# Opening of a hybrid encoder block: the first products of one token block put ahead of the second block's transposes

## The chip, the core and the metric

The kernel runs on one core of a Trainium2 chip. The metric is the device time in microseconds of one execution. The core has a matrix engine (PE), a vector engine (DVE), a scalar engine (ACT), a general engine (POOL) and a queue engine (SP) that issues nearly all DMAs. Each engine works through its own list of instructions in order.

## What is computed

One layer of a streaming encoder over 2064 tokens (16 learned meta tokens, then 2048 inputs) of width 1024. The part that the change touches is the first line of it:

```python
p = rms_norm(h, norm_mix_pre[l]) @ w_in[l]      # h: (2064, 1024), w_in: 1024 x (512 + 1544 + 1024)
pa, pb, pc = ...                                 # columns of the three head groups
oa = rg_lru_group(...); ob = forgetting_attention_group(...); oc = rwkv7_group(...)
h = h + rms_norm(concat([oa, ob, oc]) @ w_out[l], norm_mix_post[l])
f = causal_dwconv(rms_norm(h, norm_ffn_pre[l]) @ ffn_up[l], ffn_conv[l])
h = h + rms_norm((gelu(gate) * val) @ ffn_down[l], norm_ffn_post[l])
```

`rms_norm` divides a token by the root of its mean square and multiplies by a gain. Among the columns of `w_in` are 8 for the gate of the attention group (`f_logit`).

## The kernel before

The input projection is done in three parts, each of two blocks of tokens; part 0 has the tiles of 16, 128, 128, 128 tokens (block 0, 400 tokens) and three tiles of 128 (block 1, 384 tokens). Products need the tokens turned, with the 1024 features on the partitions, and every operand is split into a high and a low half whose products are summed in three matmuls (`mm3`, lines 181 to 183).

`norm_transpose` brings one tile: a DMA into `xt` (line 131, tag `nt_x`, four buffers), the sum of squares on ACT (line 123, output to a throw-away tile `xj` of tag `stv`, two buffers), the reciprocal root by `rstd_from` on DVE (lines 90 to 92, then three rounds of lines 98 and 99, nine small instructions on one column), the scaling on DVE (line 136), eight transposes on PE (line 149, two PSUM tiles `pst`), and for each of these a copy on ACT (line 155, `xh`) and a subtraction on DVE (line 156, `xl`). With `core.root` set, `rstd_of` takes another way: two sums over half rows on ACT, one small DVE instruction, a square root on ACT (line 108) and a reciprocal on DVE (line 109). Before, it is set only in later stages.

`w_in_norm` does this for all seven tiles of part 0. Then `w_in_part` multiplies: first `w_in_gate` for both blocks (16 matmuls a block, lines 300 and 301, weights `fw` from the raw tile `fraw`, tag `stv`; `fw` lies in the pool `w` under the tag `wh`), then 24 units of 128 columns, each over both blocks (24 matmuls a block). `w_in_weights` loads a unit's columns in part 0 (`raw`, 512 KB, line 171, the same four `nt_x` buffers as the token tiles), rounds them on ACT (line 175) and subtracts on DVE (line 176), and stores both halves for the later parts (`scr_wk`, line 229). The pool `w` holds two units. Products are copied out of PSUM (lines 57 and 59) and stored (`scr_p`).

In program order the constants of the recurrences stand behind unit 12: `rwkv_consts`, `lru_consts` and the columns of `ffn_conv`, some 27 small DMAs on SP (lines 905, 952 to 955, 1442), among them the vectors that `columns` loads row by row into one tile `rows` (one buffer), turns on PE (line 911, `pscol`) and copies on DVE (line 912); that happens four times. But program order isn't what runs: the program is built with `schedule_with_timeline_sim=True`, so a planner orders each engine's instructions by its own simulated times, and it pulls the constants to the front. `tc.issue_after(ins)` keeps what is traced inside it behind `ins` on the engine of `ins`.

Of the kernel before, what the change touches and what calls it, by code (L numbers as in the profile page):

```python
# [8 lines left out]
F32 = mybir.dt.float32  # L9
F32R = mybir.dt.float32r  # L10
# [185 lines left out]
def w_in_norm(core, pools, psum, x, meta, gain, part):  # L196
    blocks = []
    for b, tl in enumerate(w_in_tokens(part)):
        t0 = tl[0][0]
        n = sum(r for _, r in tl)  # L200
        hi = pools["xn"].tile([P, KD, n], F32R, tag=f"xh{b}", name=core.n("xh"))
        lo = pools["xn"].tile([P, KD, n], F32R, tag=f"xl{b}", name=core.n("xl"))
        blocks.append((t0, n, tl, hi, lo))
    for t0, n, tl, hi, lo in blocks:
        for s, rows in tl:
            src = meta if s < META else x[s - META : s - META + rows, :]
            late = part == 1 and (s, rows) not in blocks[0][2][:2]
            after = (lambda: core.tc.issue_after(core.rounded.ins)) if late else nullcontext
            norm_transpose(core, pools, psum, src, rows, gain, [(hi, lo, s - t0, 0, rows)], after)
    return blocks  # L210


# [2 lines left out]
    return scr["wk"][c0 // P]  # L215


def w_in_weights(core, pools, w_in, c0, scr, part):

    if part == 0:  # L220
        src = w_in[:, c0 : c0 + P].rearrange("(k p) c -> p k c", p=P)
        pair = split_load(core, pools["w"], (pools["nt"], "nt_x", None), src, [P, KD, P], "w")
    else:
        core.turns += part == 2
        pl, tags = (pools["nt"], ("nt_x", "nt_x")) if core.turns % 4 > 1 else (pools["w"], ("wh", "wl"))
        pair = [pl.tile([P, KD, P], F32R, tag=tag, name=core.n(s)) for s, tag in zip(("wh", "wl"), tags)]
    for t, kept in zip(pair, w_in_kept(scr, c0)):
        t = t[:].rearrange("p k c -> p (k c)").bitcast(F32)
        core.loaded = core.nc.sync.dma_start(*((kept, t) if part == 0 else (t, kept)))
    return pair  # L230
# [51 lines left out]
def w_in_gate(core, pools, psum, w_in, blocks, scr, part):  # L282

    nc = core.nc
    c0 = 2048
    w = pools["w"].tile([P, KD, P], F32R, tag="wh", name=core.n("fw"))
    flat, kept = w[:].rearrange("p k c -> p (k c)").bitcast(F32), w_in_kept(scr, 3 * D)[0]
    if part == 0:
        raw = pools["st"].tile([P, KD, 8], F32, tag="stv", name=core.n("fraw"))
        nc.sync.dma_start(raw[:], w_in[:, c0 : c0 + 8].rearrange("(k p) c -> p k c", p=P))  # L290
        nc.vector.memset(w[:].bitcast(F32), 0.0)
        nc.scalar.activation(w[:, :, 0:8], raw[:], AF.Copy)
        nc.vector.tensor_tensor(w[:, :, 32:40], raw[:], w[:, :, 0:8], op=ALU.subtract)
        nc.sync.dma_start(kept, flat)
    else:
        nc.sync.dma_start(flat, kept)
    for t0, n, tl, hi, lo in blocks:
        ps = psum.tile([P, 512], F32, tag="mm", name=core.n("psf"))
        for k in range(KD):
            nc.tensor.matmul(ps[:, :n], w[:, k], hi[:, k], start=k == 0, stop=False)  # L300
            nc.tensor.matmul(ps[:, :n], w[:, k], lo[:, k], start=False, stop=k == KD - 1)
        a = pools["st"].tile([8, 400], F32, tag="sth", name=core.n("fa"))
        nc.scalar.activation(a[:, :n], ps[32:40, :n], AF.Copy)
        o = pools["st"].tile([8, 400], F32, tag="stl", name=core.n("fo"))
        nc.vector.tensor_tensor(o[:, :n], ps[0:8, :n], a[:, :n], op=ALU.add)
        nc.sync.dma_start(scr["f"][:, t0 : t0 + n], o[:, :n])
    yield False
    yield True


def w_in_part(core, pools, psum, w_in, blocks, scr, part):
    yield from w_in_gate(core, pools, psum, w_in, blocks, scr, part)
    units = [("c", 2056 + P * i) for i in range(8)] + [("a", P * i) for i in range(4)]
    units += [(s, c + P * i) for s, c in (("k", 1024), ("v", 1536), ("q", 512)) for i in range(4)]
    waiting = [None]

    def step(*args):

        after = w_in_step(core, pools, psum, *args, scr)
        if waiting[0]:  # L320
            waiting[0]()
        waiting[0] = after

    for kind, c0 in units[:-2]:
        w = w_in_weights(core, pools, w_in, c0, scr, part)
        for block in blocks:
            step(w, block, kind, c0)
            yield block is blocks[-1]

    last = [(w_in_weights(core, pools, w_in, c0, scr, part), kind, c0) for kind, c0 in units[-2:]]  # L330
    for block in blocks:
        for w, kind, c0 in last:
            step(w, block, kind, c0)
            yield kind == "q" and c0 == last[-1][2]
# [1821 lines left out]
def hybrid_block_kernel(ctx: ExitStack, tc: tile.TileContext, args, out):  # L2156
# [12 lines left out]
    def pool(es, name, bufs, **kw):  # L2169
        return es.enter_context(tc.tile_pool(name=name, bufs=bufs, **kw))  # L2170
# [11 lines left out]
    with ExitStack() as p1:  # L2182
# [8 lines left out]
        with ExitStack() as p1a:  # L2191
            ps_mm = pool(p1a, "ps_mm", 5, space=PSUM)
            g_pre = spread(pool(p1a, "gpre", 1), a["norm_mix_pre"], "g_pre")
            pools = {"xn": pool(p1a, "xn", 1), "nt": pool(p1a, "nt", 4), "w": pool(p1a, "w", 2), "st": pool(p1a, "st", 2)}
            sums = up_sums(core, pool(p1a, "us", 1), a["ffn_up"], scr, EARLY)
            split_out = w_out_split(core, pools["nt"], a["w_out"], scr)
            following = w_in_norm(core, pools, ps_mm, x, meta, g_pre, 0)
            for part in range(3):
                blocks = following
                if part == 0:  # L2200
                    zeros = pools["st"].tile([P, PAD], F32, tag="sth", name="zeros")
                    nc.vector.memset(zeros[:], 0.0)
                    for r in range(0, A_ROWS + C_ROWS, P):
                        nc.gpsimd.dma_start(scr["p"][r : r + P, 0:PAD], zeros[:])
                units = w_in_part(core, pools, ps_mm, a["w_in"], blocks, scr, part)
                for _ in range(READY if part == 0 else 0):
                    while not next(units):
                        pass
                if part == 0:
                    attn_consts(core)  # L2210
                    shared, core.const = core.const, rc
                    rk = rwkv_consts(
                        core, gp, ps_ae,
                        {
                            s[5:]: (v.rearrange("h d -> (h d)") if s == "rwkv_r_k" else v)
                            for s, v in a.items() if s.startswith("rwkv_")
                        },
                    )
                    lk = lru_consts(
                        core, gp, ps_ae,  # L2220
                        {
                            "conv_w": a["lru_conv_w"], "conv_b": a["lru_conv_b"], "ga_w": a["lru_gate_a_w"],
                            "ga_b": a["lru_gate_a_b"], "gx_w": a["lru_gate_x_w"], "gx_b": a["lru_gate_x_b"],
                            "lam": a["lru_lambda"],
                        },
                    )
                    core.const = shared
                    columns(core, gp, ps_ae, [a["ffn_conv"].rearrange("i (r p) -> (i r) p", p=P)], "", cw)
                    R = Rwkv(core, rp, dp, ps_rw, ps_ae, scr, rk)
                    beside = Beside(PACE)  # L2230
                i = READY + 1 if part == 0 else 1
                for whole in units:
                    if whole and i == READY + 1:
                        beside.add(recurrences(core, R, lk, a["fox_f_bias"], scr, blocks, part))
                    beside.advance()
                    if not whole:
                        continue
                    if part == 1 and i > 1:
                        next(split_out, None)
                    if part and i % 2 == 0:  # L2240
                        with tc.issue_after(core.loaded.ins):
                            next(sums, None)
                    i += 1
                run(sums) if part == 2 else None
                if part < 2:
                    following = w_in_norm(core, pools, ps_mm, x, meta, g_pre, part + 1)
# [199 lines left out]
```

## Time and profile before

| | us |
|---|---|
| three runs | 2972.48, 2979.31, 2978.02 |
| their median | 2978.02 |
| the profiled execution | 2974.88 |
| its span | 2973.2 |
| PE busy in the span | 2840.2 |
| DVE, ACT, POOL busy | 2015.4, 1505.3, 1281.3 |

The profile's page gives the busy time of each engine, a row of 40 slices of the span, the chain that ended last, and groups of instructions with their mean duration and the idle time of their engine just before them. The timeline lists instructions in order of time, with the idle time before each and what ended it in brackets. A granted clock of TensorE stands beside each stretch.

### The profile page before, as it was taken

The page shows a single profiled execution, that of the slowest core. Times are in us where ns is not written, and L with a number is a line of the kernel's source. Part 1 is how long each engine was busy: PE and PEld are TensorE (multiplying, and loading weights), DVE is VectorE, ACT ScalarE, POOL GpSimd, SP SyncE. Part 2 cuts the span into 40 slices and gives each one's busy share as a digit, 9 for nine tenths or more (in the row PEclk, how much of TensorE's full clock was granted, in tenths as well). Part 3 has the DMA queues.
Part 4 walks back from the last instruction along what each step waited for, and adds up shares of the span by engine and source line. Part 5 has one row for each costly group of instructions (what it writes and reads, how often), then busy time and mean ns, then how long its engine had stood idle before and what let it go on. Part 6 is the DMA issues. An engine that isn't in the chain of part 4 may idle for free.

```text
span 2973.2 us, 53343 instructions
## 1 busy us (share of the span) xinstructions
PE 2840.2 (96%) x18854; PEld 2448.6 (82%) x18854; DVE 2015.4 (68%) x3974; ACT 1505.3 (51%) x2937; POOL 1281.3 (43%) x1555
## 2 busy tenths in 40 slices
PE   6999999999978889999999999999999999999998
PEld 6998899889865555566568999999999999787887
DVE  5257654675678766556756988888778787646766
ACT  4246432444346555445635665666575665324333
POOL 1001121131214566766722667455655444656443
PEclk9999899999989899999999999999999999999999
DMA  6776479576654257535245665577777774436453
GB/s 219 235 233 223 156 246 322 171 240 213 209 127 95 70 130 215 125 95 130 72 133 187 204 191 173 167 230 211 205 212 219 218 199 131 155 114 222 148 171 121
DMA packets 470344, 530.52 MB, mean 178 GB/s; under 512 B 86862, under 2 KB 356888, under 8 KB 468524
## 3 DMA queue, kind: packets, MB, share of 16 engines
q1 hardware_dynamic: 469308, 526.18, 58.4%
q8 instruction: 148, 2.42, 0.3%
q14 instruction: 120, 0.98, 0.1%
q0 software_dynamic: 768, 0.93, 0.1%
HBM read 368.07 MB, written 158.90 MB: 177 GB/s over the span
## 4 chain that ended last, share of the span: by engine, by line
PE 72%; DVE 8%; DMA 7%; ACT 5%; POOL 4%; issue 3%; SPq 1%; DVEq 0%; POOLq 0%; ACTq 0%
PE psu L181 9%; PE psu L182 9%; PE psu L183 9%; PE psp L183 5%; PE psp L182 5%; PE psp L181 5%; PE psd L181 4%; PE psd L182 4%; PE psd L183 4%; PE po L733 3%; PE sc L710 2%; PE pswo L181 2%; PE pswo L182 2%; PE pswo L183 2%; PE mx L581 2%
## 5 line engine op out<-in xcount | busy, mean ns | idle before, releaser
L182 PE MATMUL psu<-xo,uw 128*128 128x344 f32 x1848 | 591.5, 320 | 0.0
L181 PE MATMUL psu<-xo,uw 128*128 128x344 f32 x1848 | 586.0, 322 | 3.5 <-DVE vb L1907 2.1
L183 PE MATMUL psu<-xo,uw 128*128 128x344 f32 x1848 | 581.9, 320 | 0.3 <-DVE uw L1716 0.3
L181 PE MATMUL psp<-xh,wh 128*128 128x384 f32 (+2 forms) x1152 | 378.3, 328 | 0.1
L183 PE MATMUL psp<-xh,wl 128*128 128x384 f32 (+2 forms) x1152 | 377.0, 328 | 0.7 <-DMA wl<-scr_wk 0.7
L182 PE MATMUL psp<-xl,wh 128*128 128x384 f32 (+2 forms) x1152 | 377.6, 328 | 0.0
L1716 DVE TENSOR_TENSOR uw<-uq,uw 128x512 fp32r<-128x512 f32 x341 | 318.8, 940 | 61.3 <-ACT uw L1715 58.3
L181 PEld LDWEIGHTS psu<-xo,uw 128*128 128x128 f32 x1848 | 345.8, 188 | 5.1 <-DVE vb L1907 3.1
L182 PEld LDWEIGHTS psu<-xo,uw 128*128 128x128 f32 x1848 | 347.2, 188 | 0.0
L183 PEld LDWEIGHTS psu<-xo,uw 128*128 128x128 f32 x1848 | 345.7, 188 | 1.1 <-DVE uw L1716 1.1
L1715 ACT ACTIVATE uw<-uq 128x512 fp32r<-128x512 f32 x462 | 288.1, 627 | 100.1 <-PE psu L183 47.3
L715 ACT ACTIVATE p<-sc,bias 128x512 f32<-128x512 f32 (+4 forms) x352 | 196.4, 590 | 166.8 <-PE sc L711 141.9
L586 DVE TENSOR_REDUCE mc<-mx 128x1 f32<-128x512 f32 (+5 forms) x352 | 191.8, 566 | 119.4 <-PE mx L581 82.9
L1855 DVE SCALAR_TENSOR_TENSOR uy<-psu,ffn_cols,uy 128x342 f32<-128x342 f32 (+1 forms) x390 | 220.6, 567 | 62.4 <-ACT uy L1853 60.7
L1716 POOL TENSOR_TENSOR uw<-uq,uw 128x512 fp32r<-128x512 f32 x121 | 184.1, 1521 | 136.7 <-ACT uw L1715 112.9
L1863 POOL TENSOR_TENSOR uy<-uy,uy 128x342 f32<-128x342 f32 (+1 forms) x132 | 144.2, 1092 | 228.7 <-DVE uy L1855 63.1
L183 PEld LDWEIGHTS psp<-xh,wl 128*128 128x128 f32 x1152 | 219.9, 191 | 7.1 <-issue 4.6
L181 PEld LDWEIGHTS psp<-xh,wh 128*128 128x128 f32 x1152 | 219.8, 191 | 4.5 <-issue 2.6
L182 PEld LDWEIGHTS psp<-xl,wh 128*128 128x128 f32 x1152 | 220.0, 191 | 3.7 <-issue 2.3
L754 POOL TENSOR_TENSOR acc<-acc,p 128x512 f32<-128x512 f32 (+3 forms) x186 | 196.5, 1059 | 48.5 <-DVE acc L754 21.4
L1716 DVE TENSOR_TENSOR fo<-u,fo 128x896 fp32r<-128x896 f32 x88 | 100.3, 1140 | 133.0 <-ACT fo L1715 132.4
L1715 ACT ACTIVATE fo<-u 128x896 fp32r<-128x896 f32 x88 | 81.2, 923 | 207.6 <-PE psd L183 122.3
(489 smaller groups left out, 6301.5 us busy)
## 6 DMA issues: line engine op xcount, KB each, us to landing
uq<-scr_us SPq DMA_DIRECT2D x220, 256.0 KB
uq<-in_ffn_up_dram SPq DMA_DIRECT2D x209, 256.0 KB
wl<-scr_wk SPq DMA_DIRECT2D x48, 512.0 KB
wh<-scr_wk SPq DMA_DIRECT2D x48, 512.0 KB
u<-scr_ff SPq DMA_DIRECT2D x88, 256.0 KB
scr_ff<-uy SPq DMA_DIRECT2D x110, 171.0 KB
raw<-in_w_in_dram SPq DMA_DIRECT2D x24, 512.0 KB
scr_wk<-wh SPq DMA_DIRECT2D x24, 512.0 KB
```

The source lines that it names most:

```text
L181: nc.tensor.matmul(out, ah, bh, start=first, stop=False, skip_group_check=more)
L182: nc.tensor.matmul(out, ah, bl, start=False, stop=False, skip_group_check=more)
L183: nc.tensor.matmul(out, al, bh, start=False, stop=last, skip_group_check=more)
L581: nc.tensor.matmul(ps[:rows, : e - a], q3[:, qo : qo + rows], k2[:, a:e], start=True, stop=not last)
L586: self.reduced = nc.vector.tensor_reduce(mc[:rows, i, ci : ci + 1], ps[:rows, : e - a], axis=AX.X, op=ALU.max)
L715: last = nc.scalar.activation(p[:rows, :w], ps[:rows, :w], AF.Exp, bias=bias[:rows, j : j + 1])
L733: mm = nc.tensor.matmul(po[at : at + 64, c0:n], v1[:rows, j], p[:rows, : n - c0], start=start and i < 2, stop=end and i + 2 >= len(group), ...
L754: eng.tensor_tensor(a, ps_[0][0][:rows, c0:n] if start and i == 1 else a, p[:rows, : n - c0], op=ALU.add)
L1715: core.nc.scalar.activation(hi, src, AF.Copy)
L1716: (eng or core.nc.vector).tensor_tensor(lo, src, hi, op=ALU.subtract)
L1855: core.conved = stt(y[:, :n], src[:, i : n + i], cw[:, 44 * i + cc : 44 * i + cc + 1], y[:, :n], op0=ALU.mult, op1=ALU.add)
L1863: core.pooled = nc.gpsimd.tensor_tensor(v[:, :n], g[:, :n], v[:, :n], op=ALU.mult)
```

## The change

- Block 0 of part 0 is normalised and turned first. The three tiles of block 1 are put on a list (`core.unturned`), and `core.turn_tile` does one of them: after unit 0's product with block 0, after unit 1's, and the third behind that. Then come the gate and the two units for block 1, and the other 22 units as before.
- The raw columns of units 0 and 1 go to a tile of their own (`rw_e` of the pool `rp`, which the recurrence uses later) instead of the `nt_x` buffers; the gate's weights go to the pool `us` instead of a `wh` buffer, so that `w` holds both units.
- `core.root` is set for the seven tiles of part 0.
- The SP instructions of the constants are put behind the last `scr_wk` store of unit 3.

```diff
 def w_in_norm(core, pools, psum, x, meta, gain, part):
...
+    core.unturned = []
+    for block in blocks:
+        for s, rows in block[2]:
+            if part == 0 and block is blocks[1]:
+                core.unturned.append((block, s, rows))
+            else:
+                tile(block, s, rows)
+    core.turn_tile = lambda: tile(*core.unturned.pop(0))
     return blocks
...
-def w_in_weights(core, pools, w_in, c0, scr, part):
+def w_in_weights(core, pools, w_in, c0, scr, part, raw=None):
+
+    src = w_in[:, c0 : c0 + P].rearrange("(k p) c -> p k c", p=P)
+    if raw is not None:
+        pair = hi, lo = [pools["w"].tile([P, KD, P], F32R, tag=s, name=core.n(s)) for s in ("wh", "wl")]
+        core.loaded = core.nc.sync.dma_start(raw, src)
+        core.rounded = core.nc.scalar.activation(hi[:], raw, AF.Copy)
+        core.nc.vector.tensor_tensor(lo[:], raw, hi[:], op=ALU.subtract)
+    elif part == 0:
...
 def w_in_gate(core, pools, psum, w_in, blocks, scr, part):
...
-    w = pools["w"].tile([P, KD, P], F32R, tag="wh", name=core.n("fw"))
+    home, tag = ("w", "wh") if part else ("us", "us")
+    w = pools[home].tile([P, KD, P], F32R, tag=tag, name=core.n("fw"))
...
 def w_in_part(core, pools, psum, w_in, blocks, scr, part):
...
+    if part == 0:
+        raws = pools["rp"].tile([P, 2, KD, P], F32, tag="rw_e", name=core.n("raw"))
+        firsts = [
+            (w_in_weights(core, pools, w_in, c0, scr, part, raws[:, i]), kind, c0)
+            for i, (kind, c0) in enumerate(units[:2])
+        ]
+        for i, block in enumerate(blocks):
+            gate(*block)
+            yield i > 0
+            for w, kind, c0 in firsts:
+                step(w, block, kind, c0)
+                if i == 0:
+                    core.turn_tile()
+                yield i > 0
+            while core.unturned:
+                core.turn_tile()
+        del units[:2]
...
+            core.root = True
             following = w_in_norm(core, pools, ps_mm, x, meta, g_pre, 0)
...
-                for _ in range(READY if part == 0 else 0):
+                for i in range(READY if part == 0 else 0):
                     while not next(units):
                         pass
+                    core.root = core.root and not i
+                    if i == 4:
+                        begun = core.loaded.ins
                 if part == 0:
                     attn_consts(core)
                     shared, core.const = core.const, rc
+                    p1c = ExitStack()
+                    p1c.enter_context(tc.issue_after(begun))
                     rk = rwkv_consts(
...
+                    p1c.close()
                     R = Rwkv(core, rp, dp, ps_rw, ps_ae, scr, rk)
```

More of the change, by code (lines that the diff above doesn't have):

```diff
@@ L203, in w_in_norm, with tile @@
         blocks.append((t0, n, tl, hi, lo))
[L204 to L209, printed above, removed]
+    def tile(block, s, rows):
+        t0, _, _, hi, lo = block
+        src = meta if s < META else x[s - META : s - META + rows, :]
+        late = part == 1 and (s, rows) not in blocks[0][2][:2]
+        after = (lambda: core.tc.issue_after(core.rounded.ins)) if late else nullcontext
+        norm_transpose(core, pools, psum, src, rows, gain, [(hi, lo, s - t0, 0, rows)], after)
+    core.unturned = []
[6 more added lines that the diff above has]
+    core.turn_tile = lambda: tile(*core.unturned.pop(0))
     return blocks
@@ L215, in w_in_kept @@
     return scr["wk"][c0 // P]
-def w_in_weights(core, pools, w_in, c0, scr, part):
-    if part == 0:
-        src = w_in[:, c0 : c0 + P].rearrange("(k p) c -> p k c", p=P)
+def w_in_weights(core, pools, w_in, c0, scr, part, raw=None):
[6 more added lines that the diff above has]
+    elif part == 0:
         pair = split_load(core, pools["w"], (pools["nt"], "nt_x", None), src, [P, KD, P], "w")
@@ L296, in w_in_gate, with products @@
         nc.sync.dma_start(flat, kept)
-    for t0, n, tl, hi, lo in blocks:
+    def products(t0, n, tl, hi, lo):
         ps = psum.tile([P, 512], F32, tag="mm", name=core.n("psf"))
@@ L306, in w_in_gate @@
         nc.sync.dma_start(scr["f"][:, t0 : t0 + n], o[:, :n])
-    yield False
-    yield True
+    return products
 def w_in_part(core, pools, psum, w_in, blocks, scr, part):
-    yield from w_in_gate(core, pools, psum, w_in, blocks, scr, part)
+    gate = w_in_gate(core, pools, psum, w_in, blocks, scr, part)
     units = [("c", 2056 + P * i) for i in range(8)] + [("a", P * i) for i in range(4)]
@@ L322, in step @@
         waiting[0] = after
+    if part == 0:
[15 more added lines that the diff above has]
+        del units[:2]
+    else:
+        for block in blocks:
+            gate(*block)
+        yield False
+        yield True
     for kind, c0 in units[:-2]:
@@ L2194, in hybrid_block_kernel @@
             pools = {"xn": pool(p1a, "xn", 1), "nt": pool(p1a, "nt", 4), "w": pool(p1a, "w", 2), "st": pool(p1a, "st", 2)}
-            sums = up_sums(core, pool(p1a, "us", 1), a["ffn_up"], scr, EARLY)
+            pools["us"], pools["rp"] = pool(p1a, "us", 1), rp
+            sums = up_sums(core, pools["us"], a["ffn_up"], scr, EARLY)
             split_out = w_out_split(core, pools["nt"], a["w_out"], scr)
+            core.root = True
             following = w_in_norm(core, pools, ps_mm, x, meta, g_pre, 0)
```

## The prediction

> **What bounds the kernel now.** I read the page's busy shares first, then its 40 slices, then stretches of the opening, and last the timelines of single engines there.
>
> ```profile
> span 2973.2 us, 53343 instructions
> PE 2840.2 (96%) x18854; PEld 2448.6 (82%) x18854; DVE 2015.4 (68%) x3974; ACT 1505.3 (51%) x2937; POOL 1281.3 (43%) x1555
> PE   6999999999978889999999999999999999999998
> ```
>
> PE is the bound: of 133 us without PE work, the first slice (74 us at six tenths) holds the largest single share, 23 by the next view. Time saved there by PE moves everything behind it. The stretches of the opening, and two later ones (columns: length, then busy us and instructions of PE, PEld, DVE, ACT, POOL, granted clock, DMA share, GB/s):
>
> ```profile
> 0.00:33.40 33.40, 9.95 (x44) 7.91 (x44) 26.15 (x134) 15.08 (x29) 11.94 (x32) 1.00 0.62 185
> 33.40:36.60 3.20, 3.15 (x16) 2.92 (x17) 3.11 (x10) 1.39 (x3) 0.00 (x0) 1.00 1.05 400
> 36.60:60.00 23.40, 23.40 (x134) 23.40 (x133) 10.20 (x24) 12.91 (x19) 0.00 (x0) 1.00 0.73 224
> 280.00:300.00 20.00, 10.94 (x247) 9.95 (x245) 15.88 (x50) 16.25 (x34) 5.54 (x12) 0.72 0.68 216
> 300.00:320.00 20.00, 19.02 (x142) 15.83 (x143) 17.80 (x43) 13.74 (x28) 4.87 (x9) 0.59 0.08 24
> ```
>
> From 33.4 us on PE is full. Before it PE works 9.95 of 33.4 us, on transposes and constants alone. What PE waits for there:
>
> ```profile
> 10.36 1.00 PE L149 MATMUL pst<-ident,xt 16*128 16x16 f32 x8 [10.36 <-DVE rs L99]
> 12.77 0.27 PE L911 MATMUL pscol<-ident,rows 22*128 22x22 f32 x1 [1.41 <-DMA rows<-in_rwkv_ln_b_dram]
> 13.82 1.97 PE L149 MATMUL pst<-ident,xt 128*128 128x128 f32 x8 [0.78 <-DVE xt L136]
> 18.02 0.26 PE L911 MATMUL pscol<-ident,rows 16*128 16x16 f32 x1 [2.23 <-DMA rows<-in_lru_lambda_dram]
> 18.20 1.97 PE L149 MATMUL pst<-ident,xt 128*128 128x128 f32 x8
> 22.90 1.94 PE L149 MATMUL pst<-ident,xt 128*128 128x128 f32 x8 [2.73 <-DVE xt L136]
> ...
> 33.45 3.42 PE L149 MATMUL pst<-ident,xt 128*128 128x128 f32 x16 [4.51 <-DVE lruv L1456]
> 36.62 0.43 PE L300 MATMUL psf<-xh,fw 128*128 128x400 f32 x1
> ```
>
> Block 0 is the first four groups of line 149; the fourth ends at 24.8 us, yet the first product starts at 36.62, behind all seven tiles. What holds the tiles is seen on ACT:
>
> ```profile
> 7.19 1.06 ACT L123 ACTIVATE xj<-xt 128x1024 bf16<-128x1024 f32 x1 [0.41 <-DMA xt<-in_x_dram]
> ...
> 10.73 1.06 ACT L123 ACTIVATE xj<-xt 128x1024 bf16<-128x1024 f32 x1 [0.42 <-DMA xt<-in_x_dram]
> 11.69 0.18 ACT L123 ACTIVATION_READ_ACCUMULATOR xj<-xt 128x1 f32 x1
> 11.78 0.32 ACT L155 ACTIVATE xh<-pst 128x64 fp32r<-128x64 f32 x2
> 17.34 1.06 ACT L123 ACTIVATE xj<-xt 128x1024 bf16<-128x1024 f32 x1 [5.24 <-DMA xt<-in_x_dram]
> 18.40 1.06 ACT L155 ACTIVATE xh<-pst 128x512 fp32r<-128x512 f32 x2
> ```
>
> All four tiles of block 0 have landed by 10.73. Then ACT sits 5.24 us in front of the fifth tile, a block 1 tile, while tile 1, turned at 15.8, waits for its copy until 18.40. The chain of waits says why that tile is late:
>
> ```profile
> 3.13 7.92 DMA rows<-in_rwkv_mu_dram
> ...
> 13.60 3.64 DMA xt<-in_x_dram
> ```
>
> A 4 KB vector issued at 3.13 landed at 11.05, behind the tokens: SP's transfers pass in order, and the constants stand in SP ahead of the fifth tile, which is issued at 13.60 and needs 3.64 us.
>
> **The change, part by part.** Prices from the groups of the opening and of the stage that already takes roots on ACT:
>
> ```profile
> L136 DVE SCALAR_TENSOR_TENSOR xt<-xt,rs,g_pre 128x1024 f32<-128x1024 f32 x5 | 6.4, 1273 | 0.0
> L156 DVE TENSOR_TENSOR xl<-pst,xh 128x512 fp32r<-128x512 f32 x8 | 5.4, 682 | 0.1
> L155 ACT ACTIVATE xh<-pst 128x512 fp32r<-128x512 f32 x8 | 4.4, 584 | 1.6 <-PE pst L149 1.6
> L98 DVE SCALAR_TENSOR_TENSOR rs<-rs 128x1 f32<-128x1 f32 x17 | 3.5, 216 | 0.0
> L99 DVE SCALAR_TENSOR_TENSOR rs<-rs 128x1 f32<-128x1 f32 x17 | 2.6, 157 | 0.0
> L175 ACT ACTIVATE wh<-raw 128x1024 fp32r<-128x1024 f32 x1 | 1.1, 1057 | 0.4 <-DMA raw<-in_w_in_dram 0.4
> L1610 ACT ACTIVATE jk<-pswo 128x512 bf16<-128x512 f32 x17 | 10.0, 588 | 8.9 <-PE pswo L183 8.5
> L1610 ACT ACTIVATION_READ_ACCUMULATOR jk<-pswo 128x1 f32 x17 | 3.3, 195 | 0.0
> L108 ACT ACTIVATE rs<-rs x25: 276/285/297, 1534.8 to 2967.9; 128x1 f32<-128x1 f32 x25
> L108 ACT ACT_TABLE_LOAD  x3: 1283/1283/1283, 1533.5 to 2760.2; - x3
> L911 PE MATMUL pscol<-ident,rows 22*128 22x22 f32 (+3 forms) x4 | 1.2, 308 | 3.7 <-DMA rows<-in_lru_lambda_dram 2.2 <-DMA rows<-in_rwkv_ln_b_dram 1.4
> L176 DVE TENSOR_TENSOR wl<-raw,wh 128x1024 fp32r<-128x1024 f32 x1 | 1.2, 1226 | 0.3 <-ACT wh L175 0.3
> L1051 ACT ACTIVATE rwwa<-rwraw,rwkv_om x3: 503/507/512, 114.8 to 242.0; 128x256 f32<-128x256 f32 x3
> ```
>
> (1) *Roots on ACT.* DVE loses three rounds of 0.216 + 0.157 = 1.1 us a tile; the three small instructions ahead of them become one and a reciprocal. ACT's squares grow from 1.06 + 0.18 to 2 x (0.588 + 0.195) = 1.57 us, and it gets a root of 0.285 and one table load of 1.283, which falls on tile 0. ACT thus does more, 0.6 us a tile; only the shorter chain on DVE pays.
>
> On that load the Trainium skill has a harder rule: "ScalarE: Activation LUTs", section "What ACT_TABLE_LOAD costs", says that a switch to another set costs 1283 ns and a drain of about 1380 more. The rows show the 1.283 alone, with the root beginning right behind it (1533.5 to 1534.8). With the page's drain the sum below would be 1.4 us less.
>
> (2) *When does block 0 stand?* I go along ACT. Tile 0's squares begin when the meta tokens land; tile 3 lands at 10.73 unless the raw weights pass before it. After 10.73 the shortest way is: squares 1.57, root and reciprocal with hand-overs 0.7, scaling 1.27, transposes 1.97, the last copy 0.58, the last subtraction 0.68, and some 0.1 for each of five hand-overs: 18.0. ACT is also behind by then: the work in front of tile 3's squares pushes them by some 2 us (table load 1.28, three roots 0.85), so 19.5 as the near end. The far end has the copies of tiles 1 and 2 (4 x 0.58) and unit 0's rounding (1.06) in front of tile 3's root: 3.4 later, 22.9. I take the middle, 21. The raw weights ahead of the tokens would cost two tile steps (7.19 to 10.73 is two tiles, 3.5 us), which the far end holds. `fraw` needs the throw-away buffer of tile 2's squares, so it is issued at about 12 and lands behind two raws by some 18 to 19, in time.
>
> (3) *What PE has to do from there.* At 33.45 two tiles were left to turn (3.42 us); at 21 three are (3 x 1.95 = 5.85): 2.4 us more. The four `pscol` transposes, 1.2 us, lay in PE's idle time and now lie in the full stretch. So 33.45 - 21 - 2.4 - 1.2 = 8.8 us; with the two ends of (2), 10.3 and 6.9.
>
> (4) *Block 1.* Matmuls pass every 23.40/134 = 0.175 us, so the gate (16) and two units (48) over block 0 give 11.2 us of cover: until 32 at the earliest. Tile 4's buffer is free at 11.4 (tile 0 turned), those of 5 and 6 about 3 and 5 us later; with 3.64 us to land and two raws and `fraw` in front, tile 6 lands by about 23 and is scaled by 27. Cover 5 us, cost nothing; without it, up to the 5.24 us that ACT once sat.
>
> (5) *Weights.* Units 0 and 1 keep both halves of `w` until block 1's products are done. Unit 2's rounding and subtraction (1.06, and 1.23 on DVE) then run beside unit 1 over block 1 (24 x 0.175 = 4.2 us): nothing, unless its raw tile is late; it is loaded some 15 us ahead. The gate's move to `us` and the raws' to `rp` use buffers that nobody wants before part 1 and the recurrences: nothing. The 2.5 MB of stores to `scr_wk` come some 12 us earlier, and SP, in order, holds whatever stands behind a store that waits for its halves; what stands there are raws of units 2 and later, early by more than 10 us.
>
> (6) *Constants.* SP's 27 small issues move behind unit 3's store. Unit 3's half comes free when both first units are through: 21 + 11.2 + 5.85 + 11.2 = 49, and the rounding and subtraction make it about 52 us. The first reader of them is at 114.8 (line 1051), so 40 us of cover remain after some 20 us for the batch. Behind them in SP queue the raws of units 5 and on (four buffers, over 25 us ahead) and `scr_p` stores (two buffers and five PSUM tiles). The price is on PE: a `pscol` transpose stands in PE's list and everything behind it waits if its rows are late. Before, the waits were 1.41 and 2.23 and about nothing, 3.7 us on an idle PE. Bounds: 0, if the planner places them late enough, and 3.7. I take 1.4, nearer to nothing, since the batch is now small between large transfers and PE has other work ready.
>
> Sum: 8.8 - 1.4 = 7.4 us, between 6.9 - 3.7 = 3.2 and 10.3. Against the profiled execution, 2974.88, that gives 2967.5. The median of the three runs is 2978.02, 3.1 us above it; against it the time is 2970.6.
>
> **Rivals.** About 0.2% (6 us) is what a measurement here can tell from none.
>
> *A. ACT is held again, now by a raw tile or tile 4 in front of block 0's copies.* For it: the 5.24 us above, which came from the planner putting the fifth tile's squares before tile 1's copy. Against: constants no longer stand in front of that tile. One such wait takes 5.24 off: 2.2 us gained, 2975.8.
>
> *B. Slower: the constants stop a full PE.* Place: the four `pscol` in PE's list at 52 to 80 us. Price: if each load takes what the first one took, 7.92, and nothing covers it, 31.7 - 8.8 = 22.9 slower, 3001. It decides from 8.8 + 6 = 14.8 us of waits in all, 3.7 each. For it: SP passes in order, and 0.73 of the DMA time is taken there; against: the waits before were 1.41 and 2.23.
>
> *C. More than forecast.* PE's three earlier groups show that DVE's queue, not only ACT, held tiles (2.73 <-DVE xt, 4.51 <-DVE lruv); with constants gone it may be quick throughout. Block 0 at 18.0 and no `pscol` wait: 33.45 - 18 - 3.6 = 11.8, 2966.2, and with two roots earlier some 13, 2965.
>
> *D. The clock.* After the gap at 280 to 300 the granted clock is 0.72 and then 0.59; in the opening it is 1.00 although PE idles 10.36 us there. If the products, which now follow a sparse stretch instead of 3.42 us of dense transposes, ran their first 3.4 us at half clock, 1.7 us would go: 2972.3.
>
> The rule beside D is that of the Trainium skill, "TensorE: Matmul & The Clock Gate", section "Part 1: The HAM clock gate (the "warmup" mystery)": after an idle window of about 3.4 us the clock halves until a busy window has passed. The opening's rows speak against it, the later ones for it.
>
> **How the numbers follow.** The forecast has 0.60 (2967.7 to 2974.8 on its own bounds; three quarters or more of it beyond 6 us), A 0.12, B 0.10, C 0.13, D 0.05. Faster by over 0.2%: most of the forecast, 0.51, and C, 0.13: 0.64. Within 0.2%: the rest of the forecast 0.09, A and D: 0.26. Slower: B, 0.10. The range holds the forecast, A, C and D and half a spread of the runs above A: 2963 to 2979.
>
> **What would show it.** Right: the first `psf` at about 21 us with PE full from there; no waits of ACT on `xt` over 1 us ahead of block 0's copies; roots at 8 to 15 us with one table load; `pscol` at 55 to 80 us with less than 2 us of PE idle in all; units 2 and on without a wait for `wl`. Wrong: a PE wait at the seam between unit 1 over block 0 and the gate over block 1, `pscol` waits above 3.7 each, or the stages behind 100 us in another order with another length of the hole at 280 to 300.

## The result, and the profile after

The changed kernel took 2987.89 us (median of 17 runs), the kernel before in the same session 2978.10: ratio 1.0029, with a 95% interval from 1.0018 to 1.0040. It is 9.8 us slower. The forecast of 2970.6 was wrong in size and in sign.

The busy shares and PE's slices of the page after, as shown of before:

```profile
span 2988.6 us, 53295 instructions
PE 2858.3 (96%) x18854; PEld 2460.5 (82%) x18854; DVE 2015.5 (67%) x3925; ACT 1511.2 (51%) x2960; POOL 1288.6 (43%) x1555
PE   7999999999978889999999999999999999999998
```

The span grew by 15.4 us and PE's busy time by 18.1, with the same 18854 matmuls: PE did not wait more in sum, its matmuls took longer. The first slice rose from 6 to 7: the opening did gain, and the loss lies elsewhere.

I followed the same matmuls of PE through both timelines, by their count within each product. In the median the changed kernel is 3.2 us ahead over 55 to 135 us. At 865 us that lead is gone (between 1.3 us ahead and 2.2 behind, by product); from 910 us it is behind by about 12, from 1240 us to the end by 13 to 15. Three places matter.

**The opening.** PE's timeline after:

```profile
20.73 0.70 PE L317 MATMUL psf<-xh,fw 128*128 128x400 f32 x1
21.23 0.54 PE L181 MATMUL psp<-xh,wh 128*128 128x400 f32 x1
...
24.62 0.42 PE L181 MATMUL psp<-xh,wh 128*128 128x400 f32 x1
24.88 0.34 PE L182 MATMUL psp<-xl,wh 128*128 128x400 f32 x1
...
29.97 1.03 PE L149 MATMUL pst<-ident,xt 128*128 128x128 f32 x8
...
35.22 1.91 PE L149 MATMUL pst<-ident,xt 128*128 128x128 f32 x16
...
41.17 0.45 PE L317 MATMUL psf<-xh,fw 128*128 128x384 f32 x1 [4.05 <-ACT xh L155]
...
42.48 0.69 PE L181 MATMUL psp<-xh,wh 128*128 128x384 f32 x1 [0.68 <-DVE xl L156]
43.08 0.69 PE L318 MATMUL psf<-xl,fw 128*128 128x384 f32 x1
...
48.36 0.47 PE L181 MATMUL psp<-xh,wh 128*128 128x384 f32 x1
48.67 0.34 PE L182 MATMUL psp<-xl,wh 128*128 128x384 f32 x1
```

The first product starts at 20.73 (forecast: 21). The last tile of block 0 had its root on ACT at 14.39, but its scaling on DVE came behind the subtraction for unit 1's weights:

```profile
16.40 1.21 DVE L235 TENSOR_TENSOR wl<-raw,wh 128x1024 fp32r<-128x1024 f32 x1
17.54 1.28 DVE L136 SCALAR_TENSOR_TENSOR xt<-xt,rs,g_pre 128x1024 f32<-128x1024 f32 x1
```

At the seam of the two blocks PE waits 4.05 us for ACT's copies. ACT's timeline shows what held them:

```profile
6.99 1.28 ACT L108 ACT_TABLE_LOAD   x1
8.29 0.29 ACT L108 ACTIVATE rs<-rs 16x1 f32<-16x1 f32 x1
...
35.37 0.63 ACT L453 ACTIVATE rwr<-rwk,fb 8x400 f32<-8x400 f32 x1 [3.67 <-DMA rwk<-scr_f]
36.01 1.28 ACT L454 ACT_TABLE_LOAD   x1
37.31 0.54 ACT L454 ACTIVATE rwr<-rwr 8x400 f32<-8x400 f32 x1
37.86 1.28 ACT L455 ACT_TABLE_LOAD   x1
39.15 0.54 ACT L455 ACTIVATE rwr<-rwr 8x400 f32<-8x400 f32 x1
39.60 2.00 ACT L155 ACTIVATE xh<-pst 128x512 fp32r<-128x512 f32 x4
```

Lines 453 to 455 are the further work on the gate of block 0. They come earlier with the gate's product, wait 3.67 us for a DMA, load two tables, and the four copies of block 1's last two tiles stand behind them.

**The constants.** Their issues on SP begin at 62 us; the transposes on PE come far later, and so does the first reader of them (line 1091, 1051 before). One row each from SP's timeline and from the views of the tiles `pscol` and `rwwa`:

```profile
62.43 0.94 SPq L945 DMA_DIRECT2D rows<-in_rwkv_mu_dram  x1
L951 PE MATMUL pscol<-ident,rows x4: 220/232/272, 142.4 to 165.1; 22*128 22x22 f32 x1, 16*128 16x16 f32 x1, 128*128 128x128 f32 x1, 4*128 4x4 f32 x1
L1091 ACT ACTIVATE rwwa<-rwraw,rwkv_om x9: 348/508/510, 143.4 to 889.9; 128x256 f32<-128x256 f32 x8, 128x64 f32<-128x64 f32 x1
```

The first reader runs at 143.4 instead of 114.8. By about 550 us the recurrence has caught up; this costs nothing at the end.

**From the recurrence to the attention, 866 to 960 us.** What PE waits for between 860 and 1000 us (total, times, longest): three lines of before, then the first three of after.

```profile
PE sc L710 <- DMA q<-scr_qh: 5.5, 1, 5.5
PE mx L581 <- DVE q L498: 5.0, 1, 5.0
PE rps L1348 <- DVE rstate L1352: 1.2, 4, 0.4
```
```profile
PE rps L1388 <- DVE rstate L1392: 8.3, 2, 5.6
PE mx L621 <- DVE mc L626: 5.5, 4, 3.0
PE sc L750 <- ACT p L755: 4.7, 2, 3.4
```

In after the round of the recurrence waits, in before the attention's first products do. In sum PE waits no longer in after: of these 140 us it idles 30.1 in before and 26.4 in after.

The timelines there, DVE's before and then DVE's and PE's after:

```profile
866.91 0.29 DVE L1352 COPY rstate<-rps 128x128 f32<-128x128 f32 x1 [0.70 <-PE rps L1348]
...
870.48 0.25 DVE L1352 COPY rstate<-rps 128x128 f32<-128x128 f32 x1
...
871.47 0.48 DVE L496 MEMSET q<- 64x512 f32 x1
```
```profile
866.93 0.48 DVE L536 MEMSET q<- 64x512 f32 x1 [0.16 <-issue]
...
872.40 0.48 DVE L518 MEMSET q<- 64x512 f32 x1
872.92 0.29 DVE L1392 COPY rstate<-rps 128x128 f32<-128x128 f32 x1
```
```profile
873.26 0.38 PE L1388 MATMUL rps<-rstate,rwgt 64*64 64x64 f32 x2 [5.57 <-DVE rstate L1392]
...
876.71 0.70 PE L1388 MATMUL rps<-rstate,rwgt 64*64 64x64 f32 x8 [2.75 <-DVE rstate L1392]
...
877.54 0.49 PE L621 MATMUL mx<-k,q 128*128 128x144 f32 x1
...
879.62 0.38 PE L1388 MATMUL rps<-rstate,rwgt 64*64 64x64 f32 x2
```

Two orders differ. On DVE the attention's preparations (`q`, `k`) now stand ahead of four copies of the recurrence's state. On PE the attention's first products (`mx`) now stand inside a round of the recurrence; before, that round is finished first. The change touches neither; the planner wrote both orders anew.

### The profile page after: what moved, and what is told of

Its sections match the earlier page's. It is cut to its first block, busy times and chain, and to the rows that moved or that the text cites. A ratio compares the mean times of both kernels' runs of the same rounds, so it can differ in the third digit from the quotient of the medians.

```text
span 2988.6 us, 53295 instructions
## 1 busy us (share of the span) xinstructions
PE 2858.3 (96%) x18854; PEld 2460.5 (82%) x18854; DVE 2015.5 (67%) x3925; ACT 1511.2 (51%) x2960; POOL 1288.6 (43%) x1555
## 4 chain that ended last, share of the span: by engine, by line
PE 70%; DVE 9%; DMA 8%; ACT 5%; POOL 3%; issue 3%; SPq 2%; DVEq 0%; POOLq 0%; ACTq 0%
PE psu L181 9%; PE psu L182 9%; PE psu L183 9%; PE psd L181 4%; PE psd L182 4%; PE psd L183 4%; PE psp L182 4%; PE psp L183 4%; PE psp L181 4%; PE po L773 3%; PE sc L750 2%; PE pswo L181 2%; PE pswo L182 2%; PE pswo L183 2%; PE mx L621 2%
```

## The experiments

The table gives, for each kernel, its lead at 55 to 135 us and the difference of the spans (its profile against the profile of before; minus is ahead or shorter), and its median against that of before in its own session. Two edits on the constants and the gate occur in several kernels: "hold" puts the constants' SP issues behind unit 3's store, "gate held" puts the gate's ACT work (lines 453 to 455) behind the last copy of a tile.

| run | kernel | lead at 55-135 | span | median to before | ratio (95%) |
|---|---|---|---|---|---|
| after | the change | -3.2 | +15.4 | +9.8 | 1.0029 (1.0018-1.0040) |
| e1_pin | after, state copies first | -4.3 | -6.4 | -2.1 | 0.9995 (0.9986-1.0004) |
| e2_hold | before, hold alone | -2.3 | -9.4 | -10.9 | 0.9959 (0.9945-0.9973) |
| e3_free | after without hold | +2.5 | -3.9 | -11.7 | 0.9960 (0.9946-0.9974) |
| e4_gate | after, gate held | -9.5 | -5.9 | -6.3 | 0.9979 (0.9967-0.9990) |
| e5_roots | before, roots alone | -0.5 | +1.9 | +1.7 | 1.0009 (0.9998-1.0020) |
| e6_free_gate | after, gate held, no hold | -8.8 | -11.9 | -23.0 | 0.9929 (0.9913-0.9944) |
| e7_hold2 | before, hold at unit 1 | -1.3 | -4.9 | -8.5 | 0.9970 (0.9955-0.9985) |
| e8_noroot | after without roots | -3.0 | -0.3 | -1.8 | 1.0000 (0.9989-1.0010) |
| e9_pin_delay | e1_pin and 12 memsets | -2.7 | +3.6 | -1.3 | 0.9998 (0.9988-1.0008) |
| e10_before_delay | before and 12 memsets | +2.3 | +4.2 | +1.8 | 0.9999 (0.9987-1.0010) |
| e11_pe_order | after, `mx` held on PE | -2.7 | +1.6 | -1.9 | 0.9995 (0.9985-1.0006) |

A single profiled execution can lie some 9 us from the median of its kernel (e6_free_gate: 2963.0 profiled, 2954.2 median), so verdicts go by medians and places by profiles.

**Is it the new order at 866 us?** e1_pin:

```diff
-            at = Attn(core, ...)
+            with tc.issue_after(R.states[23].ins):
+                at = Attn(core, ...)
```

> The changed kernel with one planner choice held: the twelve DVE instructions that prepare the attention's buffers stand behind the four state copies of the recurrence's sixth block, where they stand in the kernel before; in the changed kernel they stand ahead of them. Seam theory (the opening gained about 3 us, and the whole loss comes from this order at 866 to 910 us): the first products 3 us earlier than before all the way, 2975 us, 0 to 4 us under the kernel before. Constants theory (the held constants start the recurrence 15 us late, and that ends it late): no change from the changed kernel, 2988, 10 us over the kernel before.

2975.3 us: 12.6 of the kernel's time came back (11.8 with each kernel against the before of its session), and with it all of the loss. So the loss goes when the order at this seam, with all that the planner does behind it, is another. Which part of that order counts is asked by e9_pin_delay to e11_pe_order.

**The parts of the change.** e2_hold (before, with the constants held), e3_free (after, without that), e4_gate (after, the gate's ACT work behind the copies), in that order; the lines that set `begun` and `core.opened` are left out:

```diff
+                    p1c.enter_context(tc.issue_after(begun))    # e2_hold: added to before
...
-                    p1c.enter_context(tc.issue_after(begun))    # e3_free: taken from after
...
-    nc.scalar.activation(a, x, AF.Abs, bias=core.fb[:])    # e4_gate
+    with core.tc.issue_after(core.opened) if t0 == 0 else nullcontext():
+        nc.scalar.activation(a, x, AF.Abs, bias=core.fb[:])
```

> The kernel before with one part of the change alone: the SP instructions of the constants behind unit 3's weight store. Its order at the seam of recurrence and attention is that of the kernel before. Constants theory: the recurrence starts late and the time is 8 to 13 us over the kernel before. Seam theory: the late start is caught up, as in the changed kernel by 550 us, and the time is within 4 us of the kernel before; the opening itself may gain, since the fifth token tile no longer stands behind the constants in SP.

> The changed kernel with the constants not held. Both theories let the loss go, since the order at the seam is that of the kernel before and the recurrence starts early: 2974 to 2979. If the loss stays (2985 and over), neither holds and the roots or the split of the opening carry it.

> The changed kernel with the first gate block's ACT instructions (which waited 3.67 us for a DMA and then loaded two tables, 35.4 to 39.7 us) put behind the last copy of the opening's tiles. The order at the seam is that of the kernel before here too. Opening theory: the PE wait of 4.05 and 0.68 us at 37 to 42 us goes, and with it the 5 us at half clock behind it (about 2.5 us lost): unit 2's products 9 to 11 us ahead of the kernel before instead of 3.2. Seam theory on top: 2966 to 2971 us. Constants theory: 2980 to 2985.

In e2_hold the recurrence's first product starts 15.7 us late (at 169.87 us for 154.15), and yet the kernel gains 10.9: holding the constants is no loss. In e3_free, without the hold, the opening loses its lead (2.5 us behind before), and still the kernel gains 11.7. Both gains are larger than either theory allowed. In e4_gate PE's wait of 4.05 us at the seam of the blocks is down to 0.35 and the lead grows by 6.3 to 9.5 us, as expected; the time, 2971.07 us, is at the upper edge of what the seam theory had. ACT shows the order reversed:

```profile
36.68 2.07 ACT L155 ACTIVATE xh<-pst 128x512 fp32r<-128x512 f32 x4 [4.16 <-PE pst L149]
38.60 0.61 ACT L455 ACTIVATE rwr<-rwk,fb 8x400 f32<-8x400 f32 x1
```

But of that lead (16.8 us at 865 us in its profile) only 9 are left at 1240 us. So e4_gate shows what held the seam of the blocks, while the three ends are in no relation to the three leads.

**Roots, both mends, another place of the hold.** e5_roots sets `core.root` around block norms in before; e8_noroot takes it from after; e6_free_gate joins e3_free and e4_gate; e7_hold2 is e2_hold with unit 1 (`i == 2`) for unit 3 (`i == 4`).

```diff
+            core.root = True       # e5_roots: before;  e8_noroot takes this line from after
             following = w_in_norm(core, pools, ps_mm, x, meta, g_pre, 0)
+            core.root = False      # e5_roots
```

> The kernel before with one part of the change: the roots of the opening's token tiles (part 0) by ScalarE; order of products, constants and weights as before. Opening theory (what the tiles save is what the whole kernel saves): the two opening table loads and the shorter roots bring PE's first product from 33.45 to some 31-32 us, so 1 to 3 us faster at the end. Order theory (between 860 and 1150 us, where the recurrence ends and the attention begins, an order that the planner writes sets the time, and it changes with any edit ahead of it): the lag at 55-135 us is -1 to -3 us, but the lag at the end differs from it by 3 us or more, either way (between -12 and +5).

> The changed kernel with two edits: the recurrence's constants are no longer held behind a unit's weights, and the first gate block's Abs on ScalarE is put behind the last tile's copy. Opening theory: without the hold the opening lost 5.6 us of its lead (lag +2.4 against -3.2 us at 55-135); with the gate's ScalarE work behind the copies it gains some 6 us over that; so a lag of about -4 at 55-135 and the same at the end: about 2973 us. Order theory: lag -4 at 55-135 us as well, but at the end between -12 and 0 with no relation to it; the order at 866-873 us has the state copies first, so nothing of the 12 us is there.

> The kernel before with the constants held behind unit 1's weights instead of unit 3's (the run with the hold alone came out at 2966.4 us). Hold theory (the hold itself is worth 11 us, since the constants' transfers and transposes leave the opening): the same 2966 within 3 us, the recurrence starting some 15 us late as there. Order theory: the lag at 55-135 us is -2 as there, and the end differs from that run by 3 us or more.

> The changed kernel with the opening's roots by VectorE's iteration as before. Opening theory: block 0's tiles stand 1-3 us later than in the changed kernel (products from 22-24 us instead of 20.73), but without the table loads ScalarE has 2.6 us less in front of block 1's copies, so PE's stall of 4.05 us at the seam of the blocks shrinks to 1-3 us; lag at 55-135 us -2 to -5. Order theory: at 866-873 us the state copies are ahead of the attention's preparations again, so the 12 us lost in the changed kernel are not lost: 2965-2977 us, whatever the roots do in the opening.

Roots alone are worth 0.5 us in the opening and nothing that can be told at the end, less than both theories had. e6_free_gate is the best version, faster than both kernels: 2954.2 us, 0.71% below before. Its lead was twice the expected 4 us; its 23 us are more than any lead explains, and where they come from is not shown. e7_hold2 came out within 3 us of e2_hold by the medians (2968.7 and 2966.4), as the hold theory had it; by the profiles they are 4.5 apart, as the order theory had it. Between the two it decides little. e8_noroot is as fast as before and has the state copies first; that it isn't slow agrees with e1_pin. Its first product starts only at 23.71 us, and yet its lead is 3.0 against 3.2 with the roots.

**Is it the six late microseconds of the state copies?** e9_pin_delay and e10_before_delay put twelve VectorE memsets ahead of the same four copies; both have the dependence of e1_pin. What stands behind, the planner writes anew: in both it moves two of the attention's `sc` products into the round of the recurrence (at 881.4 and 877.1 us).

```diff
+            with self.core.tc.issue_after(self.last.ins):
+                for _ in range(12):
+                    late = nc.vector.memset(idle[:], 0.0)
+            slow.enter_context(self.core.tc.issue_after(late.ins))
```

> The pinned changed kernel (state copies ahead of the attention's preparations, 2975.3 us) with twelve VectorE memsets of 64x512 on a tile that nobody reads, put right ahead of the same four state copies: some 6 us more VectorE work (12 x 0.48 us) in the place where the changed kernel had its preparations. It computes the same. Seam theory (the time is lost because the state copies, on which PE and the rest of the recurrence wait, come 6 us late at 867 us): 2985 to 2990 us, 9 to 15 us more than the pinned kernel, PE waits for rstate of 5 us and more at 866-880 us. Rival (only the added VectorE work counts, or it hides): 2974 to 2982 us. Rival (the pin helped by other orders that it brought along later): no change against the pinned kernel within 3 us.

> The kernel before, with the same twelve memsets ahead of the same four state copies (and the attention's preparations behind them, as they are in it anyway); opening as before, the same result computed. Seam theory: 9 to 15 us slower than before, 2986 to 2993 us, without anything of the change in it. Rival (the added VectorE work is hidden or costs only itself): 0 to 6 us slower.

The view of the tile in e10_before_delay, and the first and the last of the four copies in its timeline of DVE:

```profile
L1350 DVE MEMSET rwidle<- x12: 485/485/485, 864.5 to 873.7; 64x512 f32 x12
```
```profile
874.08 0.22 DVE L1360 COPY rstate<-rps 128x128 f32<-128x128 f32 x1
...
878.93 0.29 DVE L1360 COPY rstate<-rps 128x128 f32<-128x128 f32 x1 [2.43 <-PE rps L1356]
```

The copies came 7.2 to 8.5 us later than in before (866.91 and 870.48), in e9_pin_delay 14.5 to 17.4 us later than in e1_pin, and nothing measurable of it was left: 2975.8 against 2975.3 for e1_pin, 2978.87 against 2977.12 for before. In e10_before_delay the recurrence is 14.6 us behind at 921 us, and the attention's scores only 1.1 us at 1121. Both rivals of e9_pin_delay fit. The seam theory as I had put it has fallen: late copies cost nothing here, with the order that the planner writes behind them.

**Then it is the order behind them.** e11_pe_order leaves DVE's preparations ahead of the copies, as in after, and pins an order on PE alone:

```diff
-                nc.tensor.matmul(ps[:rows, : e - a], q3[:, qo : qo + rows], k2[:, a:e], ...)
+                with core.tc.issue_after(core.outs[11]) if self.firsts <= 5 else nullcontext():
+                    nc.tensor.matmul(ps[:rows, : e - a], q3[:, qo : qo + rows], k2[:, a:e], ...)
```

> The changed kernel with only TensorE's order put back at the place where its plan forks from the pinned one: the first five mx products of the attention are issued behind the recurrence's round that is then under way. On VectorE the attention's preparations stay ahead of the four state copies, as in the changed kernel. Theory now (after the delays cost nothing: not the late copies lose the 12 us, but the order behind them, in which PE takes attention products ahead of a round of the recurrence and is then held by both): 2973 to 2979 us, back to the pinned kernel within 3 us, although PE still waits 5 us and more for rstate at 867-880 us. Rival (VectorE's order at the seam, the preparations ahead of the copies, costs the 12 us): 2985 to 2991 us as in the changed kernel.

2974.58 us, back to e1_pin within 0.7. DVE's preparations are still first and PE waits just as long, but the round of the recurrence is now finished before the first `mx`. At 877 us lies the fork, the first place where the lists of after and e11_pe_order differ. Up to there the lists of PE, DVE, ACT and POOL are the same in both; behind it the planner wrote all four anew. Waits, DVE's and PE's timelines of e11_pe_order:

```profile
PE rps L1390 <- DVE rstate L1394: 9.4, 3, 5.6
```
```profile
872.71 0.29 DVE L1394 COPY rstate<-rps 128x128 f32<-128x128 f32 x1
```
```profile
883.10 1.12 PE L1426 MATMUL rps<-rww,rwsc 128*64 128x64 f32 x16
884.15 0.49 PE L623 MATMUL mx<-k,q 128*128 128x144 f32 x1
```

With the same wait of 5.6 us and the same late copies, 13.3 us less (11.6 with each kernel against the before of its session): the order from this point on is what the changed kernel lost its time by. The pin stands on PE; whether PE's list alone does it, or the lists of the other engines behind it too, is not told apart. In every other kernel of the table, too, the round is finished before the first `mx`, and none of them is slower than before by more than 1.8 us. They differ in more than that, so this agrees and proves nothing by itself.

Where the time goes is seen in the same 3869 products of PE, from the fork to the 11000th of its list (columns as in the prediction; after's row holds one more, of its edge). First before, then after, e1_pin and e11_pe_order:

```profile
868.97:1553.05 684.08, 626.88 (x3869) 396.06 (x3870) 442.89 (x1044) 362.72 (x717) 395.17 (x576) 0.96 0.47 119
```
```profile
877.54:1566.51 688.97, 640.90 (x3870) 405.17 (x3870) 433.96 (x1025) 363.47 (x719) 397.14 (x576) 0.94 0.46 116
```
```profile
867.44:1547.03 679.59, 622.58 (x3869) 394.30 (x3870) 444.62 (x1043) 364.17 (x718) 396.53 (x576) 0.95 0.47 119
```
```profile
878.93:1553.85 674.92, 628.89 (x3869) 397.38 (x3870) 430.16 (x1021) 364.01 (x717) 397.44 (x576) 0.95 0.46 118
```

After comes to the fork 8.6 us later than before, and e11_pe_order later still; but e11_pe_order makes that up behind the fork, and after does not. After's stretch is 14.1 us longer than that of e11_pe_order, and 12.0 of these are busy time of PE on the same products. Against before, PE is busy 14.0 us longer and idles 9.1 less (48.1 for 57.2): slower matmuls, not longer waits. The granted clock is the lowest of the four, and more so between 860 and 1000 us, where it is 0.77 in after and 0.88, 0.85 and 0.82 in before, e1_pin and e11_pe_order. Whether the clock is a cause or only follows the new rhythm of gaps was not tried. Nor is it settled which of the later swaps in PE's list matters; from the fork on the two lists differ in many places.

## Why the prediction was wrong, point by point

- **The step that failed: "Time saved there by PE moves everything behind it."** The sum ended at PE's lead, took everything behind the opening to move rigidly with it, and had no term for the planner. In fact the opening's lead of 3.2 us was gone by 865 us, and the order that the planner wrote from the fork on cost 12.6 us (e1_pin) or 13.3 (e11_pe_order), more than the whole forecast gain of 7.4. I had named "the stages behind 100 us in another order" among what would make me wrong, and priced it nowhere; all four rivals lie in the first 100 us. Rival B foresaw the sign by another mechanism: PE's waits, over the first 140 us and from there to 170, hold none for `rows`.
- **(1) Roots: right, but for one load.** One table load of 1.28 at 6.99 with the root right behind it at 8.29. Of the drain of some 1380 ns that the Trainium skill states ("ScalarE: Activation LUTs", "What ACT_TABLE_LOAD costs") there is no trace here either: 0.02 us lie between. What the sum lacks is the way back: two loads stand in front of block 1's copies (36.01 and 37.86), and without the roots one (e8_noroot, at 39.01). Alone the roots change nothing that can be told at the end (e5_roots, 1.0009).
- **(2) Block 0: the time right,** 20.73 for 21, **the way to it in part luck.** I went along ACT and took the middle of two ends. ACT was at the near end (the last tile's root at 14.39); the rest was lost on DVE, where unit 1's subtraction stood ahead of the scaling until 17.54.
- **(3) PE's work: wrong in two terms, both too dear.** The three tiles took 1.03 + 1.91 = 2.9 us of PE and not 5.85, since eight transposes took 1.0 in the dense stretch; the `pscol` transposes fell at 142 to 165 us and not here.
- **(4) "Block 1 costs nothing": failed.** The cover of 5 us was counted for the token DMAs alone. What I did not move in my head was the gate's further work on ACT, which comes with the gate: 3.67 us for its DMA and two table loads in front of the copies. PE lost 4.05 + 0.68 us. That is near the price without cover, up to 5.24, but by another wait than the one that price was taken from; e4_gate gave it back (6.3 us with what hangs on it).
- **(5) Weights: no wait of PE.** PE's waits of the first 140 us hold none for a weight; DVE's work on them is what held block 0 in (2).
- **(6) Constants: the price within its bounds, the cover wrong.** PE waited for none of them, with 1.4 forecast between 0 and 3.7. The "40 us of cover" counted the transfers. But PE's list has the first `pscol` only at 142.4 us, 28 us behind the old first reader, and since one `rows` buffer serves all four batches, the second is loaded behind it. The recurrence made up for the late start; e2_hold, with the same late start, ended 10.9 us ahead of before.
- **D, the clock: true, and twice.** From 21.23 to 24.62 ten matmuls start 0.34 apart instead of 0.18: 1.6 us, for 1.7 forecast. From 43.08 to 48.36 sixteen start 0.33 apart instead of 0.175: 2.5 us, behind the 4.05 us wait. What the Trainium skill states ("TensorE: Matmul & The Clock Gate", "Part 1: The HAM clock gate (the "warmup" mystery)") is half the clock after an idle window of some 3.4 us, until PE has been busy for as long. The second stretch has such a wait in front and lasts 5.3 us, longer than that; the first lasts 3.4 us and has only waits of 1.60 and 2.46 us close before it. The prediction took the opening's shown clock of 1.00 as speaking against D; but there a tile's transposes take 1.94 to 1.97 us, in the dense stretch after 1.03, so PE was slow in the opening already.
- **The opening's balance:** 33.45 - 20.73 = 12.7; 0.5 more for three tiles in 2.9 us where two took 3.42; less 4.7 for the waits and 4.1 for the clock: 4.4. Measured 3.2.

## What to carry to other kernels

Where a planner writes the order, an edit at the head of a program can rewrite the order at its tail: a forecast needs a term for that, and here kernels with leads between -9.5 and +2.5 us ended between -23 and +10. Compare the lists of instructions of old and new kernel first, find the fork, and pin the order there by one dependence before judging the edit. And when a product moves, its whole train moves: look on every other engine for what now stands ahead of the next step.

## What was not expected of the hardware

The granted clock of a stretch can miss a slow spell. The windows after for the two stretches in which matmuls started at half rate:

```profile
20.70:24.60 3.90, 3.90 (x12) 3.62 (x12) 2.64 (x7) 2.30 (x7) 0.00 (x0) 1.00 1.02 397
43.00:48.80 5.80, 5.80 (x19) 5.72 (x19) 1.18 (x4) 0.00 (x0) 0.00 (x0) 0.51 0.02 4
```

The second is shown as 0.51, the first as 1.00, although its matmuls took 0.54 us against 0.34 behind it. The spacing of equal matmuls is the surer sign. And copies that came 7.2 to 8.5 us later at 867 us, with PE waiting up to 7.5 us for one, left nothing to be measured at the end (e10_before_delay), while after and e11_pe_order, with the same wait of 5.6 us, lie 13.3 us apart: a wait by itself says little on what it costs.
